# VectorE's order written out up to the end of the gates: gated halves with six conv taps between them, diagonal masks after the modulation sums

## The chip, the core and the metric

The program runs on one core of one Trainium2 chip. The metric is device microseconds of one execution; lower is better. TensorE (PE) multiplies matrices, VectorE (DVE), ScalarE (ACT) and GpSimd (POOL) do the element-wise work, and SyncE's queue (SP) issues most of the DMAs. Each engine takes its own instructions in the order in which they were laid down, and waits on semaphores for the others.

## The reference

One decoder layer over 1024 tokens of 1024 channels, all in float32. What matters here is its first half:

```
ada = silu(c) @ ada_w + ada_b                      # six rows of 1024: shift, scale, gate, twice
h   = rmsnorm(x) * (1 + sc1) + sh1
z   = h @ w_in     # [q latent 384 | kv latent 256 | rotary key 32 | conv_in 1024 | gate_logits 2048]
q, k, v from the latents (rotary tables cos, sin from positions); causal attention -> y_attn
u   = glu_a * sigmoid(glu_b)                       # conv_in = [glu_a | glu_b], 512 channels each
u   = causal_depthwise_conv(u, width 31) + conv_b  # 31 taps for each channel
u   = silu(layernorm(u)) ;  y_conv = u @ w_conv_out
y   = (sigmoid(g_attn) * y_attn + sigmoid(g_conv) * y_conv) @ w_out ;  x = x + gt1 * y
```

A second half follows: a hierarchical mixture of experts and the last norm. The attention's mask compares positions, so the kernel builds one 128x128 mask for each of the eight diagonal blocks, and a flag that says whether the positions are such that only diagonal blocks need a mask.

## The kernel before, in words

Channels lie on partitions and tokens along the free dimension; tokens come in two halves of 512 (index `n`). Each float32 product is three matmuls of a high and a low part (`mm3`, lines 105 to 107), so each weight is first cast by ACT (high part) and subtracted by POOL (low part, `lo_part`, line 496).

The stretch that the change touches goes so. The 512 conv channels are four groups `j` of 128. For each `j` and each half `n`, `proj` accumulates `pa` (glu_a) and `pb` (glu_b) in two of four PSUM banks (tag `mm`); `glu` lets ACT take tanh of `pb` (line 540), then DVE writes the gated half into `u[j]` (line 541), which sets the bank of `pa` free. When both halves of `u[j]` are there, the convolution of that group is 31 DVE instructions over 1024 tokens, each a multiply and add into `cacc[j]` (lines 729 and 732), 124 in all. Beside them DVE computes the angles of the rotary tables (`rotary`, some forty dependent steps on 128x128 elements) and the masks and the flag (`masks`, lines 301 to 335). Then PE projects the latents (`pz`, eight token tiles) and the 2048 gate columns (`pg`, sixteen weight tiles `m` by two halves). Between the gates the program has, in the text's order: after m = 6 the layer norm's statistics (`conv_stats`: PE transposes `cacc`, DVE takes mean and variance and an inverse square root in small steps); after m = 8 and 9 `conv_act` (PE transposes back, DVE, ACT, DVE, ACT, DVE for each of eight 128x512 blocks); after m = 10 to 13 one `ada_block` each, in which DVE sums one of the four remaining rows of `ada` over eight 512 KB weight tiles (`aw`, four buffers) and reduces it (`asum`); after m = 14 `ada_rest`, where PE folds `asum` (`pa`, line 487), DVE adds the bias, PE transposes (`pada`) and SP stores the rows (`adascr`). After the gates, `conv_out` multiplies by `w_conv_out` (`pc`), and `load_lat` brings the latents back (`mln`) and transposes them (`mlT`).

What sets the order: `tc.manual_schedule(engines=...)` keeps the named engines to the order of the text inside a region. Where no region holds an engine, a scheduler plans its order from its own estimates, with the text's order as priority. In the kernel before, PE, ACT and POOL are held until `glu(0, 1)`, SP until the conv weights are loaded, and DVE only until `glu(1, 0)`; behind it `rotary` and `masks` are only tied to come later than that gated half, and everything of DVE after that, taps, gated halves, `ada_block`, statistics, is mixed by the scheduler. The pool `sb` has four-buffer tags; `buf3` is its tag `b4` with three buffers in the first `sb`; later the name `sb` means a new pool (`sb2`), where `aw` is the tag with four buffers.

Of the kernel before, what the change touches and what calls it, by code (L numbers as in the profile page):

```python
# [14 lines left out]
F32 = mybir.dt.float32  # L15
F32R = mybir.dt.float32r
BF16 = mybir.dt.bfloat16
I32 = mybir.dt.int32
U32 = mybir.dt.uint32
AF = mybir.ActivationFunctionType  # L20
OP = mybir.AluOpType
# [4 lines left out]
P = 128  # L26
T = 1024
# [11 lines left out]
CK = 31  # L39
# [12 lines left out]
def hybrid_layer(ctx: ExitStack, tc: tile.TileContext, x, c, positions, ada_w, ada_b, norm1_g,  # L52
# [5 lines left out]
    V, A, G, PE, SY = nc.vector, nc.scalar, nc.gpsimd, nc.tensor, nc.sync  # L58
# [70 lines left out]
    def run(steps):  # L129
        for _ in steps:  # L130
            pass
# [53 lines left out]
    R_N1, R_AB, R_N2, R_QG, R_KG, R_CB, R_LG, R_LB, NR = 0, 8, 56, 64, 67, 69, 73, 77, 81  # L185
# [12 lines left out]
    cols = consts.tile([P, NR], F32, name="cols")  # L198
    cw = consts.tile([P, 4, CK], F32, name="cw")
# [31 lines left out]
    def rotary():  # L231
        W = NT * NF
        pos_f = pro.tile([P, NT], F32, name="pos_f")
        V.tensor_copy(pos_f, pos_i)
        rt = buf3([P, 5, W], "rot")
        a, r, t, tt, ca = (rt[:, i] for i in range(5))
        V.tensor_tensor(a.rearrange("p (t f) -> p t f", f=NF), pos_f[:, :, None].to_broadcast([P, NT, NF]),
                        invf[:, None, :].to_broadcast([P, NT, NF]), op=OP.mult)
        MAGIC = 12582912.0

        def nearest(dst, src, unit, scale=None):
            if scale is None:
                V.tensor_scalar(dst, src, MAGIC * unit, None, op0=OP.add)
            else:
                V.tensor_scalar(dst, src, scale, MAGIC * unit, op0=OP.mult, op1=OP.add)
            V.tensor_scalar(dst, dst, MAGIC * unit, None, op0=OP.subtract)

        V.memset(tt, 0.0)
        for unit in (2.0 ** 20, 2.0 ** 8):
            nearest(r, a, unit)  # L250
            V.tensor_tensor(a, a, r, op=OP.subtract)
            f = Fraction(unit) / TWO_PI
            f -= f.numerator // f.denominator
            hi, lo = pieces(f, 12, 1)[0], 0.0
            lo = float(np.float32(float(f - Fraction(hi))))
            V.tensor_scalar(t, r, hi / unit, None, op0=OP.mult)
            V.scalar_tensor_tensor(tt, r, lo / unit, tt, op0=OP.mult, op1=OP.add)
            nearest(r, t, 1.0)
            V.tensor_tensor(t, t, r, op=OP.subtract)
            V.tensor_tensor(tt, tt, t, op=OP.add)  # L260
        parts = pieces(TWO_PI, 10, 4)

        def wrap():
            nearest(r, a, 1.0, 1.0 / (2.0 * math.pi))
            for v in parts:
                V.scalar_tensor_tensor(a, r, -v, a, op0=OP.mult, op1=OP.add)

        wrap()
        nearest(r, tt, 1.0)
        V.tensor_tensor(tt, tt, r, op=OP.subtract)  # L270
        V.scalar_tensor_tensor(a, tt, 2.0 * math.pi, a, op0=OP.mult, op1=OP.add)
        wrap()
        V.tensor_scalar(a, a, -3.1415925, 3.1415925, op0=OP.max, op1=OP.min)
        V.scalar_tensor_tensor(ca, a, -1.0, a, op0=OP.mult, op1=OP.max)
        V.tensor_scalar(ca, ca, -1.0, math.pi / 2.0, op0=OP.mult, op1=OP.add)
        return a, ca
# [37 lines left out]
    def masks():  # L314
        it = pro.tile([P, NT], I32, name="pos_t")
        int_halves(phi, plo, pos_i, it)
        pb = buf3([P, T], "posb", I32)
        SY.dma_start(pb, pos_row)
        pr = pro.tile([1, 2, NT], F32, name="pos_r")
        pbv = pb[0:1, :].rearrange("o (t p) -> o t p", p=P)  # L320
        V.tensor_reduce(pr[:, 0], pbv, axis=AX.X, op=OP.max)
        V.tensor_reduce(pr[:, 1], pbv, axis=AX.X, op=OP.min)
        pd = pro.tile([1, NT], F32, name="pos_d")
        V.tensor_tensor(pd[:, :NT - 1], pr[:, 1, 1:], pr[:, 0, :NT - 1], op=OP.is_le)
        V.tensor_reduce(vflag, pd[:, :NT - 1], axis=AX.X, op=OP.max)
        ph = buf3([P, T], "posh", I32)
        V.tensor_single_scalar(ph, pb, 16, op=OP.arith_shift_right)
        V.tensor_single_scalar(pb, pb, 65535, op=OP.bitwise_and)
        bhi, blo = f32(ph), f32(pb)
        V.tensor_copy(bhi, ph)  # L330
        V.tensor_copy(blo, pb)
        for i in range(NT):
            sl = slice(i * P, (i + 1) * P)
            tmp = pro.tile([P, P], F32, name=f"md{i}", tag="md", bufs=2)
            later_than(mdiag[:, i], bhi[:, sl], blo[:, sl], i, tmp)
# [4 lines left out]
    cvp, cvp_s = open_pool("cvp", "right")  # L340
    sa, sa_s = open_pool("sa", "left")
    sb, sb_s = open_pool("sb", "right")
# [10 lines left out]
    def buf3(shape, name, dt=F32):  # L353
        return sb.tile(shape, dt, name=name, tag="b4", bufs=3)
# [105 lines left out]
        A.copy(hT[1][0][:, k], xn[1, k])  # L460
        lo_part(hT[1][1][:, k], xn[1, k], hT[1][0][:, k])

    AB, AR, HS, CM = 10, 14, 2, 8
    asum = []

    def ada_block(b):
# [55 lines left out]
    def proj(w, n, name):  # L522
        p = ps_mm(name)
        for k in range(KD):
            proj_k(p, w, n, k)
        return p
# [11 lines left out]
    def glu(j, n, pa, pb):  # L538
        th = sa.tile([P, 512], F32, name=f"th{j}{n}", tag="th", bufs=2)
        A.activation(th, pb, AF.Tanh, scale=0.5)  # L540
        last_dve[0] = V.scalar_tensor_tensor(u[j][:, CK - 1 + n * 512:CK - 1 + (n + 1) * 512], th, 1.0, pa,
                                             op0=OP.add, op1=OP.mult).ins
# [1 line left out]
    def conv_w2(j, split=True, parts=1, raw=None):  # L544
        return (w_cols(f"wa{j}", C0 + j * P, split, parts, raw), w_cols(f"wb{j}", C0 + CC + j * P, split, parts, raw))

    order_s = ExitStack()
    order_s.enter_context(tc.manual_schedule(engines={mybir.EngineType.SP}))
    order_v, order_t = ExitStack(), ExitStack()
    ET = mybir.EngineType  # L550
    OT, OV = {ET.PE, ET.Activation, ET.Pool}, {ET.DVE}
    if OT:
        order_t.enter_context(tc.manual_schedule(engines=OT))
    if OV:
        order_v.enter_context(tc.manual_schedule(engines=OV))


    SY.dma_start(c_sb, c[0].rearrange("(p k) -> p k", k=KD))
# [50 lines left out]
    def some(g, n):  # L609
        for _ in range(n):  # L610
            next(g, None)
# [75 lines left out]
    for k in range(G0, len(pt)):  # L687
        second_half(k, pt[k])
    glu(1, 0, *pp[1, 0])
    order_v.close()  # L690
    with tc.issue_after(last_dve[0]):
        angles = rotary()
        masks()
    pp[0, 1] = [ps_mm(f"p{i}01") for i in "ab"]
    for k in range(KD):
        if k not in pt:
# [13 lines left out]
    order_t.close()  # L710
    for a, tab in zip(angles, (sinT, cosT)):
        A.activation(tab.rearrange("p a b -> p (a b)"), a, AF.Sin)
    for j in range(1, 4):
        if j > 1:
            cvw[j] = conv_w2(j)
        for n in range(2 if j > 1 else 1):
            n += j == 1
            pa = proj(cvw[j][0], n, f"pa{j}{n}")
            pb = proj(cvw[j][1], n, f"pb{j}{n}")
            glu(j, n, pa, pb)  # L720
    order_s.close()

    def conv_taps(j, k0, k1):
        if k0 == 0:
            cacc.append(cvp.tile([P, UW], F32, name=f"cacc{j}", tag="ca", bufs=4))
        a = cacc[j][:, :T]
        for k in range(k0, k1):
            if k == 0:
                V.tensor_scalar(a, u[j][:, :T], cw[:, j, 0:1], cols[:, R_CB + j:R_CB + j + 1],
                                op0=OP.mult, op1=OP.add)  # L730
            else:
                V.scalar_tensor_tensor(a, u[j][:, k:k + T], cw[:, j, k:k + 1], a,  # L732
                                       op0=OP.mult, op1=OP.add)

    for j in range(4):
        conv_taps(j, 0, CK)
    sb_s.close()


# [46 lines left out]
    def ada_rest():  # L786
        ada_columns()
        V.tensor_copy(s2row[:, 0:16], ada[:, 16:32])
        V.scalar_tensor_tensor(s2row[:, 16:24], ada[:, 32:40], 1.0, cols[:, R_N2:R_N2 + 8],
                               op0=OP.add, op1=OP.mult)  # L790
        V.tensor_copy(s2row[:, 24:32], ada[:, 40:48])
        p = ps_o("pada")
        PE.transpose(p[:32, :P], s2row, ident)
        r = sb.tile([32, P], F32, name="adar", tag="lt", bufs=4)
        V.tensor_copy(r, p[:32, :P])
        SY.dma_start(adascr, r)
# [46 lines left out]
    for m in range(16):  # L843
        w = w_cols(f"wg{m}", C0 + 2 * CC + m * P)
        for n in range(2):
            p = proj(w, n, f"pg{m}{n}")
            gt = sa.tile([P, 512], F32, name=f"gt{m}{n}", tag="gt", bufs=2)
            A.activation(gt, p, AF.Tanh, scale=0.5)  # L848
            A.dma_start(gscr[m][:, n * 512:(n + 1) * 512], gt)
        if m == 6:  # L850
            tokn = conv_stats()
        if m in (CM, CM + 1):
            conv_act(m - CM, tokn)
        if m - AB in range(4):
            ada_block(m - AB + 2)
        if m == AR:
            ada_rest()
    sb_s.close()
    sc, sc_s = open_pool("sc", "right")
    lnp, lnp_s = open_pool("lnp", "right")  # L860
# [1052 lines left out]
```

## Time and profile before

| what | value |
|---|---|
| median of 3 runs | 1093.03 us (1092.01 to 1097.25) |
| the profiled execution | 1085.18 us, span of its instructions 1083.4 us |
| PE busy | 992.9 us (92%) |
| DVE busy | 765.0 us (71%) |
| ACT, POOL busy | 436.7 us (40%), 409.6 us (38%) |
| DMA | 176.80 MB, 163 GB/s over the span |
| costliest group | 120 conv taps of DVE (line 732), 171.0 us, 1476 ns each |

The profiled execution lasted 1085.18 us, 7.85 us less than the median of the timed runs. All starts below are microseconds from the start of its span. A tile name such as `pg` stands for all its instances; a trailing h or l in a name is the high or low part. Busy times of PE are modelled, so its waits say more than its busy share.

### The profile page before, as it was taken

What the parts mean: (1) busy time and instruction counts of PE and PEld (TensorE: products, weight loads), DVE (VectorE), ACT (ScalarE), POOL (GpSimd) and SP (SyncE); (2) the same over time, 40 slices, a digit from 0 to 9 for tenths busy, and PEclk for the clock granted to TensorE, in tenths of its full rate; (3) what the DMA queues carried; (4) which work ended last, traced back from release to release, by engine and by line L of the source; (5) the groups of instructions that cost most, each with busy time, mean ns of one, the idle gap of its engine ahead of it and who ended that gap; (6) DMA issues with size and microseconds to landing.
All of it is one profiled execution on the core that took longest, in us unless ns stands there. A gap on an engine that the chain in (4) does not pass through costs nothing. (4 is left out here: it accounts for less than half of the span.)

```text
span 1083.4 us, 16818 instructions
## 1 busy us (share of the span) xinstructions
PE 992.9 (92%) x5824; PEld 832.9 (77%) x5824; DVE 765.0 (71%) x1808; ACT 436.7 (40%) x915; POOL 409.6 (38%) x354
## 2 busy tenths in 40 slices
PE   5987989999869999989999998899998999998991
PEld 3576879988757788878888877678885999987871
DVE  5379999999989804647556574964447888865575
ACT  5363312212113405457666773332223555543353
POOL 5245848724201104114343445740003455544311
PEclk9998989999989999999999999999999999998796
DMA  9902510346674219710000016684656999998843
GB/s 284 339 3 58 159 53 37 104 150 185 186 228 134 103 49 290 260 40 1 2 2 4 18 60 202 197 301 163 254 214 222 312 281 279 283 285 232 242 161 153
DMA packets 97744, 176.80 MB, mean 163 GB/s; under 512 B 14123, under 2 KB 53116, under 8 KB 97648
## 3 DMA queue, kind: packets, MB, share of 16 engines
q1 hardware_dynamic: 82736, 148.33, 41.7%
q0 software_dynamic: 9152, 16.28, 6.4%
q10 hardware_dynamic: 5760, 11.01, 2.8%
q8 instruction: 49, 0.80, 0.3%
q14 instruction: 47, 0.39, 0.1%
HBM read 145.22 MB, written 40.35 MB: 171 GB/s over the span
## 5 line engine op out<-in xcount | busy, mean ns | idle before, releaser
L732 DVE SCALAR_TENSOR_TENSOR cacc<-u,cw,cacc 128x1024 f32<-128x1024 f32 x120 | 171.0, 1476 | 0.0
L1651 PE MATMUL pe<-xT,rg 128*128 128x128 f32 (+7 forms) x512 | 77.2, 282 | 0.9 <-DVE xT L1643 0.7
L1651 PEld LDWEIGHTS pe<-xT,rg 128*128 128x128 f32 x512 | 71.0, 198 | 6.6 <-DVE xT L1643 1.1
L1646 ACT ACTIVATE xT<-xp,h2c 128x128 f32<-128x128 f32 (+7 forms) x128 | 52.4, 435 | 58.0 <-DVE xT L1643 32.2
L1651 PE MATMUL pe<-xT,ru 128*128 128x128 f32 (+7 forms) x512 | 66.1, 285 | 0.0
L1651 PEld LDWEIGHTS pe<-xT,ru 128*128 128x128 f32 x512 | 63.3, 201 | 0.0
L1680 POOL DMA_INDIRECT yscr<-ob,srci x18 | 35.8, 1987 | 57.9 <-DVE ob L1674 20.2
L105 PE MATMUL po<-woh,y 128*128 128x512 f32 x128 | 53.6, 419 | 2.3 <-DVE gm L1306 2.3
L1643 DVE TENSOR_SCALAR xT<-xp,h2c 128x128 f32<-128x128 f32 (+7 forms) x128 | 45.3, 381 | 13.0 <-ACT xT L1646 12.6
L107 PE MATMUL po<-woh,y 128*128 128x512 f32 x128 | 50.4, 393 | 0.0
L106 PE MATMUL po<-wol,y 128*128 128x512 f32 x128 | 50.3, 393 | 0.0
L848 ACT ACTIVATE gt<-pg 128x512 f32<-128x512 f32 x32 | 19.0, 595 | 66.1 <-PE pg L107 66.1
L1493 POOL TENSOR_SCALAR x1n<-x,rst 128x1024 f32<-128x1024 f32 x8 | 9.0, 1128 | 93.2 <-DVE rst L127 55.5
L474 DVE SCALAR_TENSOR_TENSOR acc<-aw,cact,acc 128x1024 f32<-128x1024 f32 x28 | 39.4, 1407 | 2.7 <-DMA aw<-in_ada_w_dram 2.5
L1638 PE MATMUL xp<-ident,xg 128*128 128x128 f32 (+7 forms) x256 | 38.9, 276 | 2.0 <-DMA xg<-xscr,si 2.0
L1674 DVE SCALAR_TENSOR_TENSOR ob<-pd,wvp,gt2b 128x512 f32<-128x512 f32 (+7 forms) x36 | 26.4, 744 | 19.3 <-DMA yscr<-ob,srci 16.9
L1630 DVE TENSOR_TENSOR rdl<-rd,rdh 128x1024 fp32r<-128x1024 f32 x30 | 36.7, 1222 | 3.0 <-ACT rdh L1629 3.0
L1056 PE MATMUL mo<-pT,V 128*64 128x128 f32 x576 | 38.5, 278 | 0.0
L1629 ACT CAST rdh<-rd 128x1024 fp32r<-128x1024 f32 x30 | 31.3, 1044 | 13.9 <-PE pd L107 13.3
L1638 PEld LDWEIGHTS xp<-ident,xg 128*128 128x128 f32 (+7 forms) x256 | 33.3, 195 | 4.1 <-DVE eid L1594 2.8
L1056 PEld LDWEIGHTS mo<-pT,V 128*64 128x64 f32 x576 | 30.8, 136 | 5.7 <-issue 5.7
L1307 POOL TENSOR_TENSOR gm<-gm 128x512 f32<-128x512 f32 x16 | 26.9, 1687 | 21.5 <-DVE gm L1306 21.0
(2072 smaller groups left out, 3093.1 us busy)
## 6 DMA issues: line engine op xcount, KB each, us to landing
aw<-in_ada_w_dram SPq DMA_DIRECT2D x32, 512.0 KB, 3.8
rg<-in_expert_w_gate_dram SPq DMA_DIRECT2D x32, 512.0 KB, 9.6
ru<-in_expert_w_up_dram SPq DMA_DIRECT2D x32, 512.0 KB, 9.7
rd<-in_expert_w_down_dram SPq DMA_DIRECT2D x32, 512.0 KB, 9.4
x<-in_x_dram SPq DMA_DIRECT2D x16, 512.0 KB, 5.7
ad<-in_ada_w_dram SPq DMA_DIRECT2D x32, 256.0 KB, 6.2
wg<-in_w_in_dram SPq DMA_DIRECT2D x16, 512.0 KB, 4.4
gscr<-gt ACTq DMA_DIRECT2D x32, 256.0 KB, 2.5
```

The costliest lines, as they stand in the source:

```text
L105: PE.matmul(ps, lh, rh, start=first, stop=False)
L106: PE.matmul(ps, lh, rl, start=False, stop=False)
L107: PE.matmul(ps, ll, rh, start=False, stop=last)
L474: V.scalar_tensor_tensor(acc, w, cact[:, k:k + 1], acc, op0=OP.mult, op1=OP.add)
L732: V.scalar_tensor_tensor(a, u[j][:, k:k + T], cw[:, j, k:k + 1], a, op0=OP.mult, op1=OP.add)
L1056: PE.matmul(po[par * DV:(par + 1) * DV, i % 4 * P:(i % 4 + 1) * P], Vt[b][:, 2 * pr + par], pTs[par][:, b * P:(b + 1) * P], start=(b == 0) ...
L1630: V.tensor_tensor(rdl, rd, f32(rdh), op=OP.subtract)
L1638: PE.transpose(p[:, c], xv[:, k, :], ident[:m, :m])
L1643: split_.append(V.tensor_scalar(xT[:, ks], p[:, c], h2c[:, 0, k:k + 1], h2c[:, 1, k:k + 1], op0=OP.mult, op1=OP.add).ins)
L1646: A.activation(xT[:, ks], p[:, c], AF.Identity, scale=h2c[:, 0, k:k + 1], bias=h2c[:, 1, k:k + 1])
L1651: PE.matmul(pa[:, o:o + m], w[:, k * P:(k + 1) * P], xT[:, k * P:k * P + m], start=(k == 0), stop=(k == KD - 1))
L1680: s_ = G.indirect_dma_start(out=yscr, out_offset=bass.IndirectOffsetOnAxis(ap=src[:m], axis=0), in_=ob[:m], in_offset=None, bounds_check=T ...
```

## The change

DVE's region now runs from the start to the end of the gates, so that all its instructions of this stretch stand in the text's order. `rotary` comes whole behind `glu(1, 0)`. The taps become a generator, and six of them are laid ahead of each gated half that follows `glu(0, 1)`; there are five such halves, so 30 of the 31 taps of group 0. The other 94 taps follow in one row (`run(taps)`), then the small inverse square roots of the latents, the statistics, `conv_act`, the four `ada_block`s and `ada_rest`. `masks` moves behind `ada_rest`: its two 4 KB tiles take slots of the tag `aw` in the later pool instead of `b4`, and its DMA of the positions is issued there; the flag `vflag`, which SP reads into a register, is computed there too. SP's region and that of PE, ACT and POOL keep their extent.

```diff
@@ masks
-        pb = buf3([P, T], "posb", I32)
+        pb = sb.tile([P, T], I32, name="posb", tag="aw", bufs=4)
...
-        ph = buf3([P, T], "posh", I32)
+        ph = sb.tile([P, T], I32, name="posh", tag="aw", bufs=4)
@@ after the second halves
     glu(1, 0, *pp[1, 0])
-    order_v.close()
-    with tc.issue_after(last_dve[0]):
-        angles = rotary()
-        masks()
+    angles = rotary()
@@ conv
+    def conv_taps():
+        for j in range(4):
+            cacc.append(cvp.tile([P, UW], F32, name=f"cacc{j}", tag="ca", bufs=4))
+            a = cacc[j][:, :T]
+            V.tensor_scalar(a, u[j][:, :T], cw[:, j, 0:1], cols[:, R_CB + j:R_CB + j + 1], op0=OP.mult, op1=OP.add)
+            yield
+            for k in range(1, CK):
+                V.scalar_tensor_tensor(a, u[j][:, k:k + T], cw[:, j, k:k + 1], a, op0=OP.mult, op1=OP.add)
+                yield
+
+    taps = conv_taps()
     for j in range(1, 4):
...
             pa = proj(cvw[j][0], n, f"pa{j}{n}")
             pb = proj(cvw[j][1], n, f"pb{j}{n}")
+            some(taps, TAPS)
             glu(j, n, pa, pb)
+    run(taps)
     order_s.close()
...
-    for j in range(4):
-        conv_taps(j, 0, CK)
@@ the gates' loop, m == AR (14)
             ada_rest()
+            masks()
+    order_v.close()
```

`some(taps, TAPS)` takes six steps of the generator (`TAPS` is 6), `run(taps)` the rest.

## Rows read from the trace of the kernel before

**Rows 1.** Busy time by stretch: length, PE, PEld, DVE, ACT, POOL, PEclk, DMA share, GB/s

```profile
87.00:100.00 13.00, 6.36 (x22) 4.91 (x21) 12.83 (x21) 4.16 (x6) 8.48 (x3) 0.81 0.35 94
...
211.00:287.00 76.00, 76.00 (x338) 62.85 (x336) 76.00 (x73) 14.38 (x23) 25.13 (x12) 1.00 0.58 177
287.00:307.00 20.00, 8.17 (x39) 6.35 (x37) 19.91 (x17) 2.01 (x3) 2.72 (x1) 0.82 0.72 202
307.00:366.00 59.00, 55.46 (x261) 44.68 (x261) 55.13 (x113) 19.19 (x31) 9.77 (x4) 0.97 0.56 173
```

**Rows 2.** Waits of PE, 60 to 420: in total, times, longest

```profile
PE cT L809 <- DVE cacc L732: 11.8, 2, 10.5
PE pb L105 <- DVE u L541: 11.7, 2, 6.6
PE cB L831 <- DVE xg L833: 2.5, 2, 1.5
PE pz L105 <- DVE u L541: 1.3, 1, 1.3
```

**Rows 3.** Timeline of DVE: start, duration, engine, line, operation

```profile
67.61 0.27 DVE L234 CAST pos_f<-pos_i 128x8 f32<-128x8 int32 x1
...
96.14 0.68 DVE L541 SCALAR_TENSOR_TENSOR u<-th,pa 128x512 f32<-128x512 f32 x1
```

**Rows 4.** Timeline of PE and ACT around the first wait

```profile
86.11 0.59 ACT L540 ACTIVATE th<-pb 128x512 f32<-128x512 f32 x1
...
97.52 0.63 PE L106 MATMUL pb<-hT0l,wb2h 128*128 128x512 f32 x1
...
101.36 0.63 PE L106 MATMUL pa<-hT0l,wa2h 128*128 128x512 f32 x1
```

**Rows 5.** DVE groups, 67.5 to 97: busy us, mean ns

```profile
L266 DVE SCALAR_TENSOR_TENSOR rot<-rot 128x128 f32<-128x128 f32 x7 | 2.0, 279 | 0.1
```

**Rows 6.** Timeline of DVE, taps with and without POOL's large instructions beside them

```profile
104.89 16.79 DVE L732 SCALAR_TENSOR_TENSOR cacc<-u,cw,cacc 128x1024 f32<-128x1024 f32 x7
...
170.25 22.80 DVE L732 SCALAR_TENSOR_TENSOR cacc<-u,cw,cacc 128x1024 f32<-128x1024 f32 x19
```

**Rows 7.** Timeline of POOL: low parts of weights

```profile
90.80 2.39 POOL L496 TENSOR_TENSOR wb2l<-wb,wb2h 128x1024 fp32r<-128x1024 f32 x1
...
105.31 20.46 POOL L759 TENSOR_TENSOR wll<-wl,wlh 128x672 fp32r<-128x672 f32 x8 [2.29 <-ACT wlh L758]
```

**Rows 8.** Timeline of DVE: one chain of small steps, then two mixed

```profile
317.44 0.17 DVE L113 TENSOR_SCALAR rstd<-vv 128x2 int32<-128x2 int32 x1
317.64 0.17 DVE L115 TENSOR_SCALAR rstd<-rstd 128x2 int32<-128x2 int32 x1
...
323.87 0.17 DVE L113 TENSOR_SCALAR rstd<-vv 128x2 int32<-128x2 int32 x1
323.94 0.15 DVE L125 TENSOR_TENSOR nwt<-nwt,rstd 128x2 f32<-128x2 f32 x1
324.07 0.17 DVE L115 TENSOR_SCALAR rstd<-rstd 128x2 int32<-128x2 int32 x1
```

**Rows 9.** DVE groups, 86 to 411: busy us, mean ns, idle before

```profile
L474 DVE SCALAR_TENSOR_TENSOR acc<-aw,cact,acc 128x1024 f32<-128x1024 f32 x28 | 39.4, 1407 | 2.7 <-DMA aw<-in_ada_w_dram 2.5
L837 DVE SCALAR_TENSOR_TENSOR xg<-ct,xg 128x512 f32<-128x512 f32 x8 | 7.4, 924 | 0.0
```

**Rows 10.** Timelines of PE, DVE and SP at the end of the gates

```profile
400.09 0.38 PE L487 MATMUL pa<-asum,fold 128*128 128x128 f32 x2
...
400.51 0.79 DVE L492 TENSOR_TENSOR ada<-pa,cols 32x32 f32<-32x32 f32 x4 [25.15 <-PE pa L487]
...
406.83 0.38 SPq L900 DMA_DIRECT2D wc<-in_w_conv_out_dram  x1
...
411.39 0.40 PE L105 MATMUL pc<-csh,wch 128*128 128x512 f32 x1
```

**Rows 11.** The `aw` tiles, 190 to 420: time from issue to landing

```profile
DMA to landing us min/median/max: 3.5/3.8/8.1
```

More of the change, by code (lines that the diff above doesn't have):

```diff
@@ L461, in second_half @@
         lo_part(hT[1][1][:, k], xn[1, k], hT[1][0][:, k])
-    AB, AR, HS, CM = 10, 14, 2, 8
+    AB, AR, HS, CM, TAPS = 10, 14, 2, 8, 6
     asum = []
@@ L545, in conv_w2 @@
         return (w_cols(f"wa{j}", C0 + j * P, split, parts, raw), w_cols(f"wb{j}", C0 + CC + j * P, split, parts, raw))
-    order_s = ExitStack()
-    order_s.enter_context(tc.manual_schedule(engines={mybir.EngineType.SP}))
-    order_v, order_t = ExitStack(), ExitStack()
+    order_v, order_s, order_t = ExitStack(), ExitStack(), ExitStack()
     ET = mybir.EngineType
     OT, OV = {ET.PE, ET.Activation, ET.Pool}, {ET.DVE}
[L552 to L555, printed above, removed]
+    order_v.enter_context(tc.manual_schedule(engines=OV))
+    order_s.enter_context(tc.manual_schedule(engines={ET.SP}))
+    order_t.enter_context(tc.manual_schedule(engines=OT))
     SY.dma_start(c_sb, c[0].rearrange("(p k) -> p k", k=KD))
@@ L719, in hybrid_layer @@
             pb = proj(cvw[j][1], n, f"pb{j}{n}")
+            some(taps, TAPS)
             glu(j, n, pa, pb)
+    run(taps)
     order_s.close()
[L723 to L733, printed above, removed]
-    for j in range(4):
-        conv_taps(j, 0, CK)
     sb_s.close()
```

## The prediction

> **What bounds the kernel now.** I read the waits of PE first, then busy time by stretch, then the timelines of DVE, POOL and SP where the waits lie. PE is busy 92% of the span and is the engine to follow. From 60 to 411 us its long waits all have one cause, DVE [rows 2]: 11.7 us in two waits for a gated half (6.6 and 5.1), 1.3 us for another, 11.8 us for the last taps, 2.5 us in `conv_act`. In that stretch DVE is never free: it works 76.0 of 76 us from 211 to 287 and 19.9 of 20 from 287 to 307, where PE has only 8.2 [rows 1]. Then it runs dry: before the bias sum at 400.51 it has waited 25.15 us for PE's fold [rows 10]. So DVE is late early and idle late, and what counts is when its pieces end, not how long they are.
>
> The first wait shows the order at fault. ACT has its tanh ready at 86.7 (86.11 + 0.59 [rows 4]); DVE writes the gated half at 96.14 [rows 3], because between 67.61 and 96.14 it works through angles and masks mixed together.
>
> A wait is paid twice. After the first one the granted clock is 0.81 from 87 to 100 [rows 1], between PE's two levels, 1.2 and 2.4 GHz. Nine matmuls from 97.52 to 101.36 start 0.427 us apart [rows 4], while 338 at full clock take 76.0 us, 0.225 each [rows 1]. About twelve run so: 12 x 0.2 = 2.4 us. I charge the same after the 5.1 us wait and 2 us after the long tap wait (clock 0.82 [rows 1]), and nothing after the wait of 1.3.
>
> **Part 1, gated halves.** Before, they cost PE 11.7 + 1.3 + 2 x 2.4 = 17.8 us. After the change the angles come alone: some forty steps of 0.28 [rows 5] are 11 us, and POOL's low parts hold some up, so about 18; 67.6 + 18 = 86, level with ACT's tanh. The first gated half then stands at about 87.5, nine us sooner. Each of the next five waits for six taps. Left alone a tap takes 22.80 / 19 = 1.20; beside POOL's large instructions 16.79 / 7 = 2.40 [rows 6], so each such instruction costs one tap's time. POOL has, up to the last gated half, four conv weights of 2.39, eight latent weights of 20.46 / 8 - 1.20 = 1.36, and four gate weights of 2.39 [rows 7]: 9.6 + 10.9 + 9.6 = 30 us. Five groups of six taps and a gated half (5 x (7.2 + 0.68) = 39 us) with these 30 make 69 us: the last half comes near 156. PE alone would need five pairs of 48 matmuls at 0.225, 54 us, from about 90. With four banks it runs ahead by two halves; laid side by side, it waits some 2 to 3 us each for the third to fifth half, 9 us in all. These waits are near the 1.3 us one, so I charge no slow clock. Gain 9; bounds 0 (POOL's work falls all into the first groups) and 17.8 (it falls outside).
>
> **Part 2, the last taps.** Masks leave the front, and the sums over `ada_w`, before mixed with the taps, now stand behind them. From 87.5: 124 taps of 1.20 (149 us), five gated halves (3), POOL 30 + 12 (five more gate weights before the end): 87.5 + 194 = 281. PE reaches the same place, the end of gate m = 6, at 287 now, so at 287 - 9 = 278. It waits 3 us instead of 11.8 and 2 for the clock: gain 11. Were part 1 to give more, PE would wait here instead; were POOL's price only shared, taps would end near 240 and both parts give 31. For parts 1 and 2 together I take 20; bounds 10 and 31.
>
> **Part 3, small chains in the text's order.** The scheduler mixed these with long instructions. Now 24 steps for the latents and some 48 for the statistics run one behind the other. A lone chain starts a step every 0.20 us (317.44 to 317.64), two mixed ones every 0.07 to 0.13 (323.87, 323.94, 324.07) [rows 8]. Against a hidden 0.1 that is 72 x 0.1 = 7 us more on DVE. In `conv_act` each block goes DVE, ACT, DVE, ACT, DVE with nothing between: 3 x 0.7 (the gated half, 0.68, has this size [rows 3]; 0.92 with POOL [rows 9]) + 2 x 0.6 (the tanh [rows 4]) = 3.3 us, 26 for eight. PE needs these results only through two transpose banks; its 2.5 us of waits [rows 2] become perhaps 6.5. Cost 4; bounds 0 and 10.
>
> The Trainium skill (VectorE: DVE Perf Modes, The DRAIN you can't avoid) says that the next instruction waits until the pipe is empty, whether or not it depends. By it mixing small steps gains nothing, part 3 costs DVE nothing and the sum would be about 4 us better. The trace speaks against it: mixed chains start in half the time [rows 8].
>
> **Part 4, the modulation sums.** This part decides. DVE's chain after the taps: 281, latents' roots 5, statistics 21 (8 x 0.8 for mean and variance, 48 x 0.2 for roots, 8 x 0.5 for scaling: rounded up), `conv_act` 26, four sums of 8 x 1.2 + two passes of 1.2 (12 each, 48; 1.41 a step before with POOL beside it [rows 9]): 381, and POOL's six remaining gate weights 14: 395. The `aw` tiles have four buffers: landing takes 3.8 us [rows 11], a step 1.3, an issue 0.4, so one tile each 5.5 / 4 = 1.4 us; against 1.2, 28 tiles wait about 5 us, partly hidden in the two passes. So the sums are ready at 395 to 400, I take 397. PE's fold stands ahead of the last gate tile, and it stood at 400.09 [rows 10]; 20 - 4 = 16 us earlier PE would be there at 384. It waits up to 13 us, unless the scheduler lays the last gate (11 us) ahead of it. `wc` is loaded only behind `adascr` (406.83), and `pc` starts at 411.39, 11.3 us after the fold [rows 10]. Fold at 397: 3 us gained; gate first: fold, rows and load 7 to 8 us after 397, so `pc` at 405, 6 to 7 gained. I take 7 lost and 16 - 7 = 9 gained; bounds 0 lost and 35 lost (landing 8.1 for every tile [rows 11]: 2.45 a tile, 28 x 1.25).
>
> **Part 5, masks.** Angles and masks had 28.5 us between 67.61 and 96.14 [rows 3]; without 11 for the angles 17 at most, and some of that is POOL's, so 13. Their tiles hold two of the four `aw` slots, over which the latents' tiles come to lie; so `mln` waits for them, and SP's read of the flag may stand ahead of loads. `conv_out` of two blocks (11 us) can cover. Cost 1; bounds 0 and 13. Attention itself needs the masks only after `conv_out`.
>
> **Sum.** 9 + 11 - 4 - 7 - 1 = 8 us. After the gates PE hardly waits until the attention is over, so a shift arrives at the end. Against the profiled execution: 1085.18 - 8 = 1077. The timed median is 7.85 us above that execution, and I forecast in its terms: 1093 - 8 = 1085.
>
> **Rivals.**
> - *The end of the gates costs nothing.* The fold goes behind the last gate or the sums are ready by 384; then 20 - 4 = 16 to 20 us remain: 1075. For it: 25 us of idle DVE [rows 10]. Against: masks leave the front, but `conv_act` and the roots take more of DVE's time than before, and POOL's price stays.
> - *It cancels.* Sums ready near 400, where the fold stood before: everything behind it is where it was. Time 1092, within 0.5%. For it: part 4's own 397 is that near.
> - *Slower: the sums come after 400.* The mechanism is the four `aw` buffers. Before, the scheduler mixed their steps with taps and gave the loads time; now 28 come in one run. From the fold at 400.09 each us later is a us lost. At 5.9 us to land (between 3.8 and 8.1) a tile takes 1.9, 28 x 0.7 = 20 us: sums at 415, less what the two passes hide, 410: 1093 + 10 = 1103. SP's queue adds to it: a load waiting for a buffer holds those behind. Against it: few other loads run then (median landing 3.8).
> - *The order is not what moves the time.* Where PE's own plan stalls elsewhere, the gated halves win and nothing else: within a few us of before. I count it with the cancelling one.
>
> The Trainium skill (SBUF — State Buffer, Who interferes with whom) makes the port that DVE and GpSimd share an exclusive lock for a whole instruction, which sets a floor under DVE's chain whatever its order. The rows of taps agree (2.40 against 1.20); the sum without the lock is the 31 of part 2.
>
> **How the numbers follow.** What a measurement here can tell from no change is about 0.5%, 5.5 us. Forecast (gain 3 to 13, 1080 to 1090): 0.42, two thirds of it (0.28) over 5.5 us. First rival 0.24, cancelling 0.14, slower 0.20. Faster: 0.24 + 0.28 = 0.52; same: 0.14 + 0.14 = 0.28; slower 0.20. Range 1071 (gain 22, the first rival and a little of part 2's upper bound) to 1101 (loss 8, half of the slower case). The forecast's own range is 1080 to 1090.
>
> **What would show it.** Right: the gated half of group 0's second half near 87.5; angles in one run; taps done near 281 (wrong if before 260 or after 295); waits of PE for line 541 below 10 us in total; `asum`'s last reduction between 390 and 400; `pc` starting at 402 to 407 against 411.39. Wrong: `asum` after 400; a wait of PE at the fold over 13 us; `mlT` starving behind the masks; new waits at line 831 over 10 us.

## The result, and the profile after

The changed kernel takes 1123.99 us (median; 1121.42 and up) against 1092.93 us for the kernel before beside it: 1.027 times as long, 95% interval 1.023 to 1.031. It is slower, and outside the range. One of its four executions took 1203.15 us and is left out of that ratio; experiment 3 comes back to it. The execution in the profile took 1125.36 us, its span is 1123.5.

This table gives the start of PE's first instruction of a kind, in us of the span, from the timelines of PE. `pg` is the first gate tile, `pa` the fold of the sums, `pada` the transpose behind it, `pc` the first product of `conv_out`, `mkp` the first after that stage. The later rows are the experiments'. Where the fold stands ahead of the last gate tile (before, 1, 5 and 10 to 12), the last column holds 5.6 us of that tile's work; in the other rows PE has no gate left there.

| kernel | pg | pa | pada | pc | mkp | pada to mkp |
|---|---|---|---|---|---|---|
| before | 210.65 | 400.09 | 405.79 | 411.39 | 464.89 | 59.1 |
| after | 201.29 | 416.39 | 418.43 | 426.69 | 495.44 | 77.0 |
| 1 halves free to be overtaken | 224.94 | 407.71 | 413.40 | 419.00 | 473.77 | 60.4 |
| 2 masks ahead of the sums | 201.15 | 429.60 | 431.64 | 436.23 | 493.86 | 62.2 |
| 4 half of the loads | 201.29 | 404.97 | 407.01 | 415.53 | 479.01 | 72.0 |
| 5 halves only | 201.36 | 396.50 | 402.19 | 407.79 | 460.34 | 58.2 |
| 6 sums among taps | 201.42 | 401.99 | 404.03 | 412.62 | 475.13 | 71.1 |
| 7 the same, masks ahead | 202.02 | 413.89 | 415.93 | 420.43 | 476.90 | 61.0 |
| 8 taps in pairs | 201.72 | 406.58 | 408.62 | 417.20 | 479.32 | 70.7 |
| 9 after, again | 202.89 | 417.91 | 419.95 | 428.42 | 495.31 | 75.4 |
| 10 as 5, again | 201.94 | 395.31 | 401.00 | 406.60 | 459.26 | 58.3 |
| 11 as 5, conv a tile later | 202.49 | 393.20 | 398.89 | 404.49 | 455.56 | 56.7 |
| 12 as 5, conv two tiles later | 201.87 | 396.99 | 402.68 | 408.28 | 459.44 | 56.8 |

The first gate tile is 9.4 us earlier. `pc` is 15.3 us late, and `mkp` 30.6, 15 more. PE's first `x1p`, 260 us further on, is 32.3 late (755.4 against 723.1). The two spans differ by 40.1: the other 8 us lie behind `x1p`, in code that the change doesn't touch (see experiments 9 to 12). PE's waits from 60 to 420 us, then from 420 to 500 (us in total, times, longest), answer to [rows 2]:

```profile
PE pa L487 <- DVE fold L485: 22.8, 1, 22.8
PE cT L802 <- DVE cacc L714: 8.5, 1, 8.5
PE pb L105 <- DVE u L541: 4.0, 1, 4.0
PE pz L105 <- DVE u L541: 3.0, 2, 2.2
...
PE mlT L889 <- ACT mln L883: 9.1, 3, 5.0
PE pc L105 <- ACT wch L898: 8.1, 2, 7.9
```

The waits for a gated half fell from 13.0 to 7.0 us, and 22.8 us at the fold are new. Busy time by stretch (columns as in [rows 1]): first gate tile to last, on to `pc`, on to `mkp`.

```profile
201.00:393.50 192.50, 183.97 (x836) 152.01 (x834) 163.21 (x207) 44.65 (x70) 35.30 (x18) 0.97 0.39 131
393.50:426.70 33.20, 1.24 (x5) 0.61 (x4) 28.50 (x46) 1.21 (x2) 0.00 (x0) 0.55 0.56 190
426.70:495.40 68.70, 58.90 (x248) 46.19 (x249) 35.70 (x79) 24.98 (x47) 17.31 (x11) 0.87 0.65 213
```

In the middle one PE has 1.24 us of work in 33.2. After that gap the granted clock of the `conv_out` stage is 0.87, between the two levels; in the kernel before the stage from `pc` to `mkp` had 1.00:

```profile
411.40:464.90 53.50, 51.01 (x250) 41.55 (x248) 30.98 (x62) 26.71 (x49) 16.57 (x11) 1.00 0.82 271
```

DVE's timeline after the change, which answers to [rows 3] and [rows 10]:

```profile
87.75 0.69 DVE L541 SCALAR_TENSOR_TENSOR u<-th,pa 128x512 f32<-128x512 f32 x1 [4.30 <-ACT th L540]
...
152.78 0.67 DVE L541 SCALAR_TENSOR_TENSOR u<-th,pa 128x512 f32<-128x512 f32 x1
...
155.41 39.86 DVE L714 SCALAR_TENSOR_TENSOR cacc<-u,cw,cacc 128x1024 f32<-128x1024 f32 x30
...
290.33 0.17 DVE L110 TENSOR_SCALAR lss<-lss 128x8 f32<-128x8 f32 x1
...
354.36 0.74 DVE L472 TENSOR_SCALAR acc<-aw,cact 128x1024 f32<-128x1024 f32 x1
...
375.43 2.61 DVE L474 SCALAR_TENSOR_TENSOR acc<-aw,cact,acc 128x1024 f32<-128x1024 f32 x2 [2.18 <-DMA aw<-in_ada_w_dram]
...
416.11 0.23 DVE L485 COPY fold<-fold 128x128 f32<-128x128 f32 x1
...
419.07 0.15 DVE L302 TENSOR_SCALAR pos_t<-pos_i 128x8 int32<-128x8 int32 x1
...
432.39 0.23 DVE L310 TENSOR_SCALAR mdiag<-md 128x128 bf16<-128x128 f32 x1
```

The first gated half stands at 87.75 (87.5 forecast; DVE had waited 4.30 us for ACT's tanh), the last at 152.78 (156). The taps end at 290.3 (281), the sums run from 354.4 to 415.7 (to 397), and the masks hold DVE from 419.07 to 432.6. Groups of DVE, 60 to 420 (busy us, mean ns, idle before), which answer to [rows 9], and the landing of the `aw` tiles, which answers to [rows 11]:

```profile
L474 DVE SCALAR_TENSOR_TENSOR acc<-aw,cact,acc 128x1024 f32<-128x1024 f32 x28 | 36.0, 1285 | 11.8 <-DMA aw<-in_ada_w_dram 11.2
...
L833 DVE SCALAR_TENSOR_TENSOR csl<-xg,csh 128x512 fp32r<-128x512 f32 x8 | 9.9, 1235 | 8.0 <-ACT csh L832 8.0
...
L830 DVE SCALAR_TENSOR_TENSOR xg<-ct,xg 128x512 f32<-128x512 f32 x8 | 5.5, 693 | 5.6 <-ACT ct L829 5.6
```

```profile
DMA to landing us min/median/max: 3.3/5.4/8.2
```

DVE waited 11.2 us for weights and 13.6 for ACT inside `conv_act`; before, 2.5 and next to nothing. In all it stood idle for 45.0 us from 60 to 415.8, where its last sum ends; before, for 9.7 us from 60 to 375.4, where it ran dry. SP's queue and one row of ACT at the end of the gates, and what SP waited for from 416 to 440:

```profile
355.13 52.31 SPq L470 DMA_DIRECT2D aw<-in_ada_w_dram  x28
...
423.73 8.60 SPq L903 DMA_DIRECT2D gc<-gscr  x2
432.37 1.86 SPq L882 DMA_DIRECT2D mln<-lscr  x4
```

```profile
426.02 0.62 ACT L898 CAST wch<-wc 128x512 fp32r<-128x512 f32 x1 [31.85 <-DVE md L308]
```

```profile
SPq L903 <- DVE md L308: 7.7, 1, 7.7
SPq L1186 <- DVE vflag L325: 2.9, 1, 2.9
```

The latents' loads in the kernel before:

```profile
408.45 1.98 SPq L887 DMA_DIRECT2D mln<-lscr  x4
```

The 28 loads go in one run that the steps pace. Behind the fold SP first waits 2.9 us to read the flag (line 1186), so the first `wc` load goes out at 423.30. The second `gc` load waits 7.7 us for the masks and leaves at 432.3, as the last of them ends, and the latents' loads (`mln`) behind it start 9.1 us after `wc` (before: 408.45 after 406.83, 1.6 us). ACT's row names a mask (`md`) as what the cast of `wc` came after; as `wc` itself had had only 2.7 us to land, and its loads take 2.6 at the least, the row doesn't settle which of the two held the cast.

### The profile page after: what moved, and what is told of

Same layout as the page of the kernel before. It is cut to its first block, busy times and chain, and to the rows that moved or that the text cites. A ratio compares the mean times of both kernels' runs of the same rounds, so it can differ in the third digit from the quotient of the medians.

```text
span 1123.5 us, 16806 instructions
## 1 busy us (share of the span) xinstructions
PE 1005.1 (89%) x5824; PEld 844.4 (75%) x5824; DVE 784.1 (70%) x1808; ACT 437.1 (39%) x915; POOL 386.3 (34%) x354
## 5 line engine op out<-in xcount | busy, mean ns | idle before, releaser
L714 DVE SCALAR_TENSOR_TENSOR cacc<-u,cw,cacc 128x1024 f32<-128x1024 f32 x120 | 192.2, 1602 | 4.1
L1646 PE MATMUL pe<-xT,rg 128*128 128x128 f32 (+7 forms) x512 | 80.8, 293 | 0.1
L1646 PEld LDWEIGHTS pe<-xT,rg 128*128 128x128 f32 x512 | 75.0, 208 | 6.0 <-issue 0.8
L1646 PEld LDWEIGHTS pe<-xT,ru 128*128 128x128 f32 x512 | 65.6, 207 | 0.0
L899 POOL TENSOR_TENSOR wcl<-wc,wch 128x512 fp32r<-128x512 f32 x8 | 10.3, 1289 | 106.9 <-ACT wch L898 102.4
L474 DVE SCALAR_TENSOR_TENSOR acc<-aw,cact,acc 128x1024 f32<-128x1024 f32 x28 | 36.0, 1285 | 11.8 <-DMA aw<-in_ada_w_dram 11.2
L1624 ACT CAST rdh<-rd 128x1024 fp32r<-128x1024 f32 x30 | 31.4, 1045 | 19.2 <-PE pd L107 18.7
L105 PE MATMUL pc<-csh,wch 128*128 128x512 f32 x64 | 28.1, 439 | 8.1 <-ACT wch L898 8.1
```

Source lines behind the costliest of these rows:

```text
L105: PE.matmul(ps, lh, rh, start=first, stop=False)
L474: V.scalar_tensor_tensor(acc, w, cact[:, k:k + 1], acc, op0=OP.mult, op1=OP.add)
L1646: PE.matmul(pa[:, o:o + m], w[:, k * P:(k + 1) * P], xT[:, k * P:k * P + m], start=(k == 0), stop=(k == KD - 1))
```

## The experiments

**1. Only the gated halves by hand** (DVE's region is closed after the loop over the halves).

```diff
...
+    order_v.close()
     run(taps)
     order_s.close()
...
-    order_v.close()
     sb_s.close()
```

> DVE's hand order ends with the last gated half; the 94 other taps, the statistics, the sums over ada_w and the masks (still written at the end) go back to the scheduler. Theory A (the 31 us come from the sums ending at 416 and from the masks behind them; the gated halves' own order is a gain): the fold is back at 385 to 400, no wait over 3 us there, conv_out starts before 405, and the time is 1075 to 1088, below the kernel before (1093). Rival B (it is the order of the halves that harms, because PE, ACT and POOL were replanned around it): still 1110 to 1125. Rival C (half and half): about 1100.

1104.54 us, 1.016 [1.008, 1.024]: missed, because the edit did another thing than meant. The 94 free taps were laid in among the halves that stand in order:

```profile
131.44 14.43 DVE L714 SCALAR_TENSOR_TENSOR cacc<-u,cw,cacc 128x1024 f32<-128x1024 f32 x12
145.79 0.68 DVE L541 SCALAR_TENSOR_TENSOR u<-th,pa 128x512 f32<-128x512 f32 x1
...
151.05 18.96 DVE L714 SCALAR_TENSOR_TENSOR cacc<-u,cw,cacc 128x1024 f32<-128x1024 f32 x14
169.94 0.67 DVE L541 SCALAR_TENSOR_TENSOR u<-th,pa 128x512 f32<-128x512 f32 x1
```

Twelve and fourteen taps instead of six ahead of a half: PE waited twice 13.6 us for halves, `pg` came at 224.94. What followed answers the question all the same: no wait at the fold, and `pada` to `mkp` 60.4 us. The losses at the end of the gates go with the hand order there.

**2. Masks ahead of the sums** (still by hand).

```diff
...
             conv_act(m - CM, tokn)
+        if m == CM + 1:
+            masks()
...
             ada_rest()
-            masks()
```

> As the changed kernel, but the masks stand ahead of the four sums instead of behind ada_rest: DVE's work to the fold is the same plus 13 us. Theory A (two costs: sums late, about 16 us, and masks between the fold and conv_out, about 15 us): the fold moves from 416 to about 425 to 429, conv_out starts 10 us after it, but conv_out's stage (start to attention's first transposes) shrinks from 69 to about 54 us: 1124 + 10 - 15 = 1115 to 1122. Rival D (masks at the end cost nothing of their own; the stage is long because all of its loads come late): the stage stays at 65 to 70 us and the time is 1132 to 1138.

1128.2 us, 1.039 [1.034, 1.045]. The fold moved from 416.4 to 429.6 and PE's wait there from 22.8 to

```profile
PE pa L487 <- DVE fold L485: 35.1, 1, 35.1
...
PE pc L105 <- ACT wch L899: 4.2, 1, 4.2
```

while `pada` to `mkp` fell from 77.0 to 62.2. So masks behind the fold cost about 15 us in the stage, and ahead of it 13 at the fold, since DVE was late there: `mkp` stands at 493.86 against 495.44. From `pc` to `mkp` it took 57.6 us instead of 68.7 (A expected 54, D 65 to 70). Neither expected time is met: the price is real (against D), and the place doesn't recover it (against A).

**3. The remaining taps of groups 1, 2 and 3 in turn.**

```diff
...
-    taps = conv_taps()
+    taps = conv_taps((0,))
...
     run(taps)
+    interleave(*(conv_taps((j,)) for j in (1, 2, 3)))
```

> As the changed kernel, but the 93 taps of groups 1 to 3 are laid in turn (1, 2, 3, 1, 2, 3) instead of one group behind the other, so no tap follows the tap that wrote its accumulator. Theory E (a tap behind its own group's tap starts about 0.1 us later: 1.31 against 1.20): 93 taps save about 10 us, the taps end at 280 instead of 290, PE's wait for them falls from 8.5 to 0 to 2, the fold stands at 406 and the time is 1112 to 1116. Rival F (the longer tap in the changed kernel is all POOL's): taps still end near 290 and the time stays 1120 to 1127.

1183.5, 1190.66, 1108.67 and 1190.98 us. In the profiled execution one rotation instruction of POOL lasted 106.53 us, and PE waited 85.9 us for the latents behind it. Timelines of POOL and DVE, then the wait of PE:

```profile
154.72 0.23 POOL L744 TENSOR_TENSOR kpe<-rt 128x16 f32<-128x16 f32 x1
...
159.47 106.53 POOL L742 TENSOR_TENSOR rt<-z,cosT 128x16 f32<-128x16 f32 x1 [4.52 <-ACT z L764]
```

```profile
158.21 107.71 DVE L715 SCALAR_TENSOR_TENSOR cacc<-u,cw,cacc 128x1024 f32<-128x1024 f32 x90
```

```profile
PE pz L105 <- ACT z L764: 85.9, 1, 85.9
```

Ninety taps follow each other 1.20 us apart, and POOL, which needs 0.2 to 1.2 us for such an instruction elsewhere, gets its turn when they are over, at 266. So the times say nothing on what taps in turn are worth to the kernel; 8 repeats it with two groups. The execution of the changed kernel at 1203.15 is late by a like amount, but its mean granted clock was 0.793, where the three late ones here have 0.91 to 0.92; no trace of it exists and experiment 9 did not meet it again: its cause stays open.

**4. Half of the `aw` loads** (each tile is loaded for an even step and used for two; the weights of the odd steps are left out of the result).

```diff
...
-            w = sb.tile(...)
-            SY.dma_start(w, adaw[:, k, b])
+            if k % 2 == 0:
+                w = sb.tile(...)
+                SY.dma_start(w, adaw[:, k, b])
```

> As the changed kernel, but in the four sums each 512 KB tile of ada_w is loaded for the even steps only and used twice (the odd tiles' weights are left out of the computation); DVE's instructions are the same. Theory G (the loads that come in one run cost the 11 us that DVE waits for them): the fold moves from 416 to about 405 and the time to about 1113. Rival H (DVE's own chain sets it, the waits are covered): less than 4 us, 1120 to 1124.

1114.51 us, 1.027 [1.020, 1.033]. The steps took the same 36.0 us and the wait for weights went:

```profile
L475 DVE SCALAR_TENSOR_TENSOR acc<-aw,cact,acc 128x1024 f32<-128x1024 f32 x28 | 36.0, 1285 | 1.0
```

The fold came 11.4 us earlier, as G expected, PE's wait there fell to 11.9, and `pc` came 11.2 us earlier. So at the fold the load rate of four buffers is worth 11 us. The ratio doesn't show it: it is that of the changed kernel, 1.027. Ratios taken beside different runs of the kernel before differ by as much: 2, with the changed kernel's markers, has 1.039. Against 2, which ran beside the same ones, 4 is 13.7 us faster and 14.9 us earlier at `mkp`.

**5. Only the halves by hand, the taps held behind them**: what 1 had meant.

```diff
...
-    run(taps)
+    order_v.close()
+    with tc.issue_after(last_dve[0]):
+        run(taps)
     order_s.close()
...
-    order_v.close()
     sb_s.close()
```

> VectorE's hand order ends with the last gated half; the 94 taps that are left are only held behind that half, and they, the statistics, the sums and the masks are the scheduler's again. Theory A (the hand order pays on the gated halves and loses at the end of the gates, by the sums in one run and by the masks): the gated halves wait for at most 8 us on TensorE as in the changed kernel, the first gate starts near 201, TensorE doesn't wait for the fold, the conv_out stage takes 54 us as before; 1080 to 1086 us. Rival C (VectorE's whole work is the bound, whatever its order): what the halves gain comes back as a longer wait for cacc ahead of the statistics; 1090 to 1094 us.

1080.19 us, 0.986 [0.977, 0.994]; repeated as 10 beside other runs, 1089.41 us, 1.001 [0.997, 1.005], just above the 1078 to 1088 expected. Together no gain that can be relied on, but the 31 us of loss are gone. The waits of PE, and DVE's row behind the fold:

```profile
PE cT L804 <- DVE cacc L714: 10.0, 1, 10.0
...
PE cT L804 <- ACT tokn L807: 3.1, 1, 3.1
PE pz L105 <- DVE u L541: 3.0, 2, 2.2
PE cB L826 <- DVE xg L828: 2.7, 1, 2.7
PE cB L826 <- ACT tokn L807: 1.8, 2, 1.6
```

```profile
396.92 0.79 DVE L492 TENSOR_TENSOR ada<-pa,cols 32x32 f32<-32x32 f32 x4 [14.40 <-PE pa L487]
```

`pg` is 9 us early, no wait at the fold is left (DVE idled 14.4 us there), and the last column of the table is 58.2 us: theory A's places are right. But of the 9 us only 3.6 are left at the fold. Not as C has it: the wait for `cacc` is 10.0 us, where it was 11.8 [rows 2]. The statistics and `conv_act` behind it, in which DVE's steps stand among the sums, make PE wait 7.6 us (for `tokn` 3.1 and 1.8, for `xg` 2.7) against 3.5, so 4 of the 6 us that went; the other 2 I haven't placed.

**6. The sums in turn with the last 54 taps, by hand**; roots ahead of them, statistics and `conv_act` four gate tiles later. **7. The same, masks ahead of the fold.**

```diff
-    AB, AR, HS, CM, TAPS = 10, 14, 2, 8, 6
+    AB, AR, HS, CM, TAPS = 10, 14, 2, 12, 6
...
-    run(taps)
+    some(taps, 40)
     order_s.close()
...
+    interleave(taps, (s for b in range(2, 6) for s in ada_block(b)))
...
-        if m == 6:
+        if m == 10:
...
-        if m - AB in range(4):
-            ada_block(m - AB + 2)
...
+            masks()        # 7 alone
             ada_rest()
-            masks()        # 7 alone
```

> All stays ordered by hand, but the 32 steps of the modulation sums are laid in turn with the last 54 taps, the roots ahead of them, and the statistics and the GELU of the conv stand four gate tiles later; the masks stay behind the fold. Theory A (the sums standing as one run behind the conv are what makes the fold late): TensorE waits neither for the fold (22.8 us in the changed kernel) nor for cacc (8.5 us), fold before 395, conv_out stage still near 69 us; 1090 to 1100 us. Rival C (VectorE's work as a whole is too much for the gates): taps and sums end after 320 and the fold moves by less than 8 us; 1112 to 1125 us.

> As the kernel with the sums woven in, and the masks stand ahead of the fold. Theory A (masks behind the fold cost the conv_out stage 15 us, ahead of it only what VectorE lacks in slack there): conv_out stage near 54 us, wait for the fold 0 to 10 us; 1078 to 1090 us, below the kernel before. Rival: the masks' 13 us on VectorE show in full at the fold; 1090 to 1100 us.

6 took 1103.31 us, 1.007 [1.003, 1.011]; 7 took 1109.68 us, 1.015 [1.008, 1.022]. PE's waits in 6, then in 7:

```profile
PE cT L806 <- DVE cacc L716: 12.4, 1, 12.4
PE pc L105 <- ACT wch L900: 8.2, 1, 8.2
...
PE pa L489 <- DVE fold L487: 3.5, 1, 3.5
```

```profile
PE pa L489 <- DVE fold L487: 16.0, 1, 16.0
PE cT L806 <- DVE cacc L716: 12.4, 1, 12.4
PE pc L105 <- ACT wch L900: 4.1, 1, 4.1
```

6 brings the fold from 416.4 to 402.0, though theory A had it before 395: with the sums among the taps, the taps no longer next to each other, and the statistics later, 14 us of the loss are gone, though the wait for `cacc` grew by 4. The edit doesn't say which of the three gave them. 7 missed: the masks moved the fold by 11.9 us and gave 10.1 back, `mkp` 476.9 against 475.1. By hand they show wherever they stand; in 5 the scheduler had them done by 382.5, and the 14.4 us of idle time that DVE had ahead of the fold came behind them.

**8. Taps of groups 1 and 2 in turn, group 3 a chain.**

```diff
...
-    taps = conv_taps()
+    taps = conv_taps((0,))
...
     run(taps)
+    interleave(*(conv_taps((j,)) for j in (1, 2)))
+    run(conv_taps((3,)))
```

> The changed kernel, but the taps of groups 1 and 2 that are left after the gated halves go in turn, as the scheduler had them; group 3 stays a chain. Theory A (a tap that follows its own predecessor starts 1.31 us after it, one that follows another group's 1.20): taps end 7 us earlier, near 283, and the fold with them; 1114 to 1119 us. Rival (the distance isn't set by the chain): nothing moves, 1121 to 1127 us. Theory P (GpSimd gets no turn while VectorE's instructions follow each other without a gap, as in one execution with three groups in turn, where a 128x16 instruction of GpSimd took 106 us): the rotation of the latents waits some 75 us, and the time comes out near 1190 us in some executions.

1111.81 us, 1.017 [1.010, 1.024]. DVE's timeline:

```profile
155.93 76.13 DVE L715 SCALAR_TENSOR_TENSOR cacc<-u,cw,cacc 128x1024 f32<-128x1024 f32 x60
...
232.82 49.81 DVE L715 SCALAR_TENSOR_TENSOR cacc<-u,cw,cacc 128x1024 f32<-128x1024 f32 x30
```

In turn 1.27 us a tap, POOL included (76.13 / 60); as a chain 1.66 (49.81 / 30), and that stretch holds more of POOL's large instructions (5 against 2). Taps ended at 282.6, 7.8 us earlier, as theory A expected, and the time is 2 us below its 1114 to 1119; the fold came 9.8 us earlier. None of its four executions was late as in 3.

**9 to 12. The changed kernel again, 5 again, and 5 with the statistics and `conv_act` one and two gate tiles later.**

```diff
-    AB, AR, HS, CM, TAPS = 10, 14, 2, 8, 6
+    AB, AR, HS, CM, TAPS = 10, 14, 2, 9, 6     # 11; 12: CM 10
...
-        if m == 6:
+        if m == 7:                             # 12: 8
```

> The changed kernel itself, beside the kernels of this group on one chip. Theory A: 1118 to 1126 us as before. Theory P (GpSimd can be kept out by VectorE's run of taps, in some executions): one execution or more some 75 us above the others, and if it is the profiled one, a rotation instruction of GpSimd that lasts tens of us within the taps.

> The kernel with only the gated halves ordered by hand, again, as the base of the next two: 1078 to 1088 us, TensorE waits 10 us for cacc at the first cT and DVE has some 14 us of idle time ahead of the fold's result.

> As the kernel with only the gated halves by hand, and the conv's statistics and GELU are issued one gate tile later (after tiles 7, 9 and 10). Theory C (after the halves VectorE's taps are the next limit, seen as TensorE's 10 us wait for cacc): one gate tile of 10.9 us lies ahead of the statistics, the wait falls to 0 to 2 us, all later markers come 8 to 12 us earlier; 1068 to 1074 us. Rival: VectorE then ends later by as much, its 14 us of idle time ahead of the fold are used up and TensorE waits there; 1078 to 1084 us.

> The same, two gate tiles later (after tiles 8, 10 and 11). Theory C: no wait for cacc and none for tokn, markers 10 to 14 us earlier than with tile 6; 1066 to 1074 us. Rival (VectorE is short of slack ahead of the fold): the wait moves to the fold, 5 us or more there; 1076 to 1084 us.

9: 1119.8 us, 1.028 [1.020, 1.037], 1113.54 to 1124.51, the same loss and no late execution, as theory A expected. 11: 1084.22 us, 0.996 [0.992, 1.000]; 12: 1085.67 us, 0.999 [0.995, 1.003]. Both expectations of theory C are missed; the times lie 0.2 and 1.7 us above the rivals' ranges, and PE waits for the fold in neither. In 11 the wait for taps only shrank from 10.0 to 7.0 and `mkp` came 3.7 us ahead of 10; in 12 another wait stood in its place:

```profile
PE cT L804 <- ACT tokn L807: 16.8, 3, 14.6
```

So 11 is the best version by its markers, 9.3 us ahead of the kernel before at `mkp`, with 6 us in the median. The end of its interval touches no change. Times spread more than markers: 5 and 10 reach the first `x1p` at 720.99 and 719.84 us, and end at spans of 1079.4 and 1090.6. From `x1p` to the end the profiles (without 3) take either 358 to 362 us (before, 4, 5, 11, 12) or 368 to 371 (the others), in code that none of these kernels alters. The granted clock differs there: from 990 to 1020 us it is 0.77 in 5 and 0.51, next to the lower level, in 10. I haven't traced why.

## Why the prediction was wrong

**Part 1** (halves, gain 9): right. 9.4 us at the first gate tile; PE's waits for line 541 are 7.0 us, 9 forecast.

**Part 2** (taps, gain 11; taps done at 281): too early by 9. The price of 1.20 us a tap came from [rows 6], where the scheduler had laid two groups' taps in turn. The change makes chains, and a tap behind its own predecessor starts 1.33 us after it, with only POOL's small instructions beside it in both cases:

```profile
155.41 25.22 DVE L714 SCALAR_TENSOR_TENSOR cacc<-u,cw,cacc 128x1024 f32<-128x1024 f32 x19
```

Nineteen took 25.22 us where [rows 6] had 22.80. Ninety-four make 12 us; experiment 8 gives back 7.8 with 60 of them. PE's wait for `cacc` stayed at 8.5, where 3 had been forecast.

Even so PE had done all its gate tiles by 393.5, where the kernel before, fold included, began `conv_out` at 411.39: parts 1 to 3 gave PE 17 us, 16 forecast. That agreement is luck. In part 2 the wait for `cacc` shrank by 3.3 us (11.8 to 8.5) and not by 8.8; **part 3** had charged PE 4 us in `conv_act`, and there its waits of 3.5 (`xg` 2.5, `tokn` 1.0) went to nothing. The 17 us were worth nothing, because of what follows.

The section that part 3 cites (the Trainium skill, VectorE: DVE Perf Modes, The DRAIN you can't avoid) also says that an instruction that isn't held starts earlier. I had left that out, and with it the section doesn't rule out what [rows 8] show.

**Part 4** is the step that failed: "the sums are ready at 395 to 400, I take 397". They were ready at 415.7. Of the 18.7 us: taps 9.4; statistics 24.6 instead of 21; `conv_act` 34.9 instead of 26 (DVE works 21.8 us where I had 17, and idles 0.7 us or more for each of ACT's answers, 13.6 us where I had 10); sums 61.3 instead of 48 and 2 of waits, with 11.2 us of waiting for weights; and 14 us set down for POOL turned out to be inside these. Part 3's pieces stood in this chain 12 us too low. Seen as a whole, DVE had `conv_act` and the sums done at 375.4 before (400.51 less 25.15 [rows 10]) and 40 us later now, and 35 of these 40 us are idle time of DVE: what was lost is the filling-in, more than time at work. One of part 4's two cases for PE did happen: the last gate tile went ahead of the fold, and `pc` stood 10.3 us behind the fold where I had 7 to 8.

The slower rival has the place (fold after 400.09) and the mechanism (28 loads in one run through four buffers; landing 5.9 us assumed, 5.4 measured). That its 410 to 415 is met is in part luck: it has 15 to 20 us of waits for weights behind a chain that is on time, and there were 11.2 behind a chain that was late. Without them, in experiment 4, the fold is still at 404.97. I gave the rival 0.20 and ended it at 1103 because it held part 4 alone.

**Part 5** (masks, cost 1; bound 13) is the other half of the loss, some 15 us. "`conv_out` of two blocks can cover" was wrong: `wc`, `gc` and the latents are all loaded behind the fold, and between them and `pc` stands what the masks hold, DVE, two `aw` slots and SP's queue. I had named SP's queue, its read of the flag and the slots and then priced them at 1 us together; SP alone waited 2.9 us for the flag and 7.7 for the masks. Experiments 2 and 7 show the price, 10 to 15 us between `pada` and `mkp`. The 77.0 of the changed kernel against 71 to 72 in 4, 6 and 8 leaves 5 to 6 us that no run explains. The longer gap of PE ahead of it lies at hand, but PE's waits at the fold of 3.5 us (6) and 15.9 us (8) leave the same 71.

The bound of part 4 (35 lost) and that of part 5 together hold the result, 1124; the range took in half of one. Nor is the masks' price had back by moving them ahead of the fold by hand: DVE had no slack there, so experiments 2 and 7 lost at the fold about what they gained behind it.

**The tests named ahead**: 87.5, angles in one run and line 541 below 10 us came; taps ended at 290, late but inside the limits of 260 and 295. `asum` between 390 and 400 and `pc` at 402 to 407 did not come (415.7 and 426.69). `asum` after 400, the wait at the fold over 13 us and `mlT` starving behind the masks (9.1 us) had been written as signs of failure, and all three came; new waits at line 831, the fourth, did not.

## What to carry to other kernels

Ordering an engine by hand is worth its gain only where that order matters (here the eight gated halves); everything else that is drawn into the same list loses the filling-in that kept the engine busy while it waited for loads and for other engines (here 45.0 us of idle DVE against 9.7). Before fixing an order, add up that engine's chain to the next point where another engine waits, with the prices of dependent neighbours, and compare it with the slack there. Work moved "behind" such a point sits on the buffers and queues of whatever starts there.

## What the runs showed of the hardware

A tap that depends on the one in front of it started 1.33 us after it ((25.22 - 1.27) / 18), one in turn with another accumulator 1.20, with the same shapes. It isn't POOL that makes the difference: the first two of the nineteen, with POOL idle from 153.1 to 157.49, take 2.60 us together, again 1.33 from start to start. `aw` tiles of 512 KB issued in a run landed in 5.4 us (median) against 3.8 when spread out [rows 11].

Least expected was experiment 3: POOL stood for 106.5 us behind 90 instructions of DVE, though each lasted 1.2 us. The Trainium skill (SBUF — State Buffer, Who interferes with whom) has the port pair that the two engines share locked for one whole instruction, and the other engine fully blocked meanwhile; read so, POOL's turn would have come after one tap. The rows of the changed kernel agree (POOL's small instructions last 0.2 or 1.2 us between taps); this one, traced once, does not, and the measurement decides: the waiting engine isn't sure of the gap between two instructions. In 8, with two groups in turn, POOL had its turn; what made the difference stays open.
